# A gate's silu: by tanh on ScalarE and an operation on VectorE, or by ScalarE's own function

## The chip, the core and the metric

One core of a Trainium2 chip runs the whole program. The metric is the device time of one execution in microseconds; the median of 3 runs of the kernel before is 2064.26 us (2061.12 to 2065.25). Engines: TensorE (PE, with its weight loads as PEld), VectorE (DVE), ScalarE (ACT), GpSimd (POOL) and SyncE (SP), which issues most of the transfers.

## The reference

A decoder trunk of two layers on 512 tokens of width 1024, all in float32. A layer is a feed-forward, a mixer, a second feed-forward and an embedding step. This case is about the two feed-forwards:

```python
def swiglu(x, w_gate, w_up, w_down):
    return (jax.nn.silu(x @ w_gate) * (x @ w_up)) @ w_down   # 1024 -> 2816 -> 1024
h += 0.5 * swiglu(rmsnorm(h))                                # twice per layer
```

silu(g) is g times the sigmoid of g, which is the same as (g / 2) (1 + tanh(g / 2)). The mixer is a recurrent block, a windowed attention and a chunked delta rule side by side.

## The kernel before

Activations stand transposed, features on the partitions and the 512 tokens along the row. Every float32 operand of a matmul is split in two (a rounded part, `hi`, and the rest, `lo`) and a product takes three matmuls. ScalarE makes the `hi` parts by a copy, VectorE the `lo` parts by a subtraction; with the weights, which are split on the chip too, this is most of the work of both.

`ffn` computes the hidden 2816 columns as 11 pairs of 256. For a pair there are two *units*, first gate (`g`), then up (`u`). A unit computes a 256 by 512 block by seven quarter products (a fast matrix product) instead of eight; its sums gather in two PSUM banks, X and Y (`pg` and `qg`, `pu` and `qu` in the rows). ScalarE and VectorE read the banks (`c11`, L553 and L554: copy and add; `p37`, L558: a copy of Y; `p16`, L562; `c21`, L565; `c12`, L568) into a tile `cg` or `cu` of two halves. Half 1 of both comes with the sign turned. A product that adds onto a bank which is being read has to wait: the sixth waits for L554, the fourth for L558.

When both units of a pair are there, `Gating` takes over:

- `scale` (L496, VectorE): gate times the row norm
- `tanh(0)`, `tanh(1)` (L500, ScalarE): one half each, 128 x 512; the scale is 0.5 for half 0 and -0.5 for half 1
- `silu` (L503, VectorE): (tanh + 1) times the gate, both halves in one instruction of 128 x 1024; this is twice the silu, with the sign of half 1 turned
- `mult` (L506, VectorE): times `cu`, both halves in one instruction; the two signs cancel
- `hi` (L510, ScalarE) and `lo` (L513, VectorE): the split for the down product

The factor 2 left over is taken out in `residual` (L585), with the 1/2 of the layer: 0.25.

In the first feed-forward the first pair is done by plain products (`plain_pair`, `PlainGating`: L524, L528, the same L503, L532 in two halves). In the other three `first_pair` does it in an order of its own. The pairs go in two rounds, 5 and 6 of them, each followed by a part of the down product. The tile `cg` exists once: the next gate unit writes it (L553) after its last reader.

Inside the loops of units the order of TensorE, ScalarE and VectorE is the order of the code. The gating of a pair is spread over the next units: scale and the two tanh late in the up unit, `silu` and `mult` early and in the middle of the next gate unit. At the start of the three combined feed-forwards the first pair's scale, tanh, tanh and `silu` all come at once, in the first gate unit of the loop, ahead of that unit's weights (L449 adds two weight blocks, L443 subtracts) and of its L554. Outside these loops a planner orders ScalarE, VectorE, POOL and the DMA issues by simulated times; TensorE's order is by hand everywhere.

Of the kernel before, what the change touches and what calls it, by code (L numbers as in the profile page):

```python
# [14 lines left out]
AF = mybir.ActivationFunctionType  # L15
ALU = mybir.AluOpType
# [46 lines left out]
def trunk(ctx: ExitStack, tc: tile.TileContext, a):  # L63
    nc = tc.nc
    V, A, G, T = nc.vector, nc.scalar, nc.gpsimd, nc.tensor
# [291 lines left out]
    def ffn(l, which, at=AT1):  # L357
        with ExitStack() as es:
# [129 lines left out]
            class Gating:  # L488
# [7 lines left out]
                    V.tensor_tensor(out=self.cg, in0=self.cg, in1=rb, op=ALU.mult)  # L496
                    self.th = ft.tile([128, 2, S], F32, tag="th", name="th")

                def tanh(self, i):
                    A.activation(out=self.th[:, i, :], in_=self.cg[:, i, :], func=AF.Tanh, scale=0.5 - i)  # L500

                def silu(self):
                    V.scalar_tensor_tensor(out=self.th, in0=self.th, scalar=1.0, in1=self.cg, op0=ALU.add, op1=ALU.mult)  # L503

                def mult(self):
                    V.tensor_tensor(out=self.th, in0=self.th, in1=self.cu, op=ALU.mult)  # L506
                    self.out = self.hilo()

                def hi(self):
# [5 lines left out]
            class PlainGating(Gating):  # L515
# [8 lines left out]
                        V.tensor_tensor(out=self.cg[:, i, :], in0=self.ps["g", i], in1=norm.rb, op=ALU.mult)  # L524
                    self.th = ft.tile([128, 2, S], F32, tag="th", name="th")

                def tanh(self, i):
                    A.activation(out=self.th[:, i, :], in_=self.cg[:, i, :], func=AF.Tanh, scale=0.5)  # L528

                def mult(self):  # L530
                    for i in range(2):
# [50 lines left out]

            def residual(d, pd):
                dt = ft.tile([128, S], F32, tag="ys", name="dt", bufs=2)
                V.scalar_tensor_tensor(out=dt, in0=pd, scalar=0.25, in1=norm.rb, op0=ALU.mult, op1=ALU.mult)  # L585
                V.tensor_tensor(out=hT[:, d, :], in0=hT[:, d, :], in1=dt, op=ALU.add)

            units = [(j, m) for j in range(NP) for m in "gu"]
# [37 lines left out]
            norm, gain = yield  # L626
# [94 lines left out]
            for r, (j0, j1) in enumerate(ROUNDS):  # L721
                us = list(range(2 * j0, 2 * j1))

                t0 = (0, 10)[r]

                def chunk(d):
                    if d not in made:
                        made[d] = grouped(loaded(src[l, d][:, t0:t0 + 8, :], 8), 8)
                    return made[d]

                made = {}
                with tc.manual_schedule(engines=inner):
                    gate, last, pair, done = None, None, None, True
                    if r == 0:
                        gate, last, pair = plain_pair() if plain else first_pair()
                        us = us[2:]
                    for u in us:
                        for i in range(1, 4):
                            load2(u + i)
                        if u + 1 < 2 * j1:  # L740
                            load(u + 1)
                        if u + 2 < 2 * j1:
                            load(u + 2)
                        unit = Unit(*units[u], pipe.pop(u))
                        w = None
                        if u + 1 < 2 * j1:
                            w = pipe[u + 1] = Weights(u + 1)

                            w.room("a")
                            w.room("b")  # L750
                            w.hi("b")
                        else:
                            raws = [loaded(src[l, d][:, t0:t0 + 8, :], 8) for d in range(2)]
                        unit.p(2)
                        if unit.m == "g" and last:
                            if not pair:
                                pair = Gating(gate.c, last.c, into(r, last.j))
                                pair.scale()
                                pair.tanh(0)
                                pair.tanh(1)  # L760
                            pair.silu()
                        if unit.m == "u" and pair:
                            pair.lo()
                            pair = None
                        if w:
                            w.s2()
                            w.lo("b")
                        else:
                            made[0] = grouped(raws[0], 8)
                        unit.p(1)  # L770
                        unit.c11()
                        if w:
                            w.s4()
                        if not done:
                            last.p(5)
                            last.c12()
                        done = False
                        if w:
                            w.room("d")
                            w.hi("d")  # L780
                            w.hi("a")
                            w.lo("d")
                            w.lo("a")
                        else:
                            made[1] = grouped(raws[1], 8)
                        unit.p(3)
                        if pair and not last:
                            norm.rows()
                        unit.p(7)
                        if w:  # L790
                            w.room("c")
                            w.hi("c")
                        unit.p37()
                        if pair:
                            if not last:
                                pair.scale()
                                pair.tanh(0)
                                pair.tanh(1)
                                pair.silu()
                            pair.mult()  # L800
                        if unit.m == "u" and u + 1 < 2 * j1:
                            pair = Gating(gate.c, unit.c, into(r, unit.j))
                            pair.scale()
                        if w:
                            w.lo("c")
                        unit.p(6)
                        if unit.m == "u" and pair:
                            pair.tanh(0)
                        unit.p16()
                        if unit.m == "u" and pair:  # L810
                            pair.tanh(1)
                        if unit.m == "g" and pair:
                            pair.hi()
                        unit.p(4)
                        unit.c21()
                        if unit.m == "g":
                            gate = unit
                        last = unit
                    last.p(5)
                    last.c12()  # L820
                    pair = Gating(gate.c, last.c, into(r, last.j))
                    pair.scale()
                    pair.tanh(0)
                    pair.tanh(1)
                    pair.silu()
                    pair.mult()
                    pair.hi()
                    pair.lo()

                if r == 0:  # L830
                    ends = {}

                    def end(d):
                        e = d // 2
                        if e not in ends:
                            raw = wrp.tile([128, 4, 128], F32, tag="wr", name="wr")
                            for i in range(2):
                                nc.sync.dma_start(out=raw[:, 2 * i:2 * i + 2, :], in_=src[l, 2 * e + i][:, 8:10, :])
                            ends[e] = halfgroup()
                            split(raw, *ends[e])  # L840
                        i = 2 * (d % 2)
                        down(pds[d], ends[e], (i, i + 1), (8, 9), False, True)
                        residual(d, pds[d])

                    pds = {}
                    for d in range(KD):
                        pds[d] = bank([128, S], "pd")
                        chunk(d)
                        if d + 1 < KD:
                            chunk(d + 1)  # L850
                        if d == KD - 2:
                            load2(2 * j1)
                            load(2 * j1)
                            pipe[2 * j1] = Weights(2 * j1)
                            pipe[2 * j1].whole()
                        down(pds[d], chunk(d), range(8), range(8), True, False)
                        if d == 0:
                            continue
                        for e in ((0, 1) if d == 1 else (d,)):
                            end(e)  # L860
# [801 lines left out]
    norm = Norm(par[:, 0, C_F1:C_F1 + 8], True)  # L1662
# [28 lines left out]
    for l in range(L):  # L1691
        pl = par[:, l, :]
        norm = rest(f, norm, pl[:, C_MX:C_MX + 8])
        f = ffn(l, 2)
        norm = mixer(l, norm, pl[:, C_F2:C_F2 + 8], f)
# [126 lines left out]
```

## Time and profile before

| | |
|---|---|
| median of 3 runs | 2064.26 us |
| the profiled execution's own time | 2064.6 us |
| its span, first to last instruction | 2062.8 us |
| mean granted TensorE clock (1 is 2.4 GHz) | 0.977 |
| TensorE busy | 1975.7 us, 96% |
| VectorE busy | 1555.2 us, 75% |
| ScalarE busy | 996.1 us, 48% |
| POOL busy | 181.1 us, 9% |

Busy time is summed over the whole span. An engine that is 75% busy can be the limit in one stage and idle in another, so the stages are looked at one by one. `out<-in` names the tiles; the same line number stands for all instructions that a line of the kernel issues. An idle time in brackets is that of the engine before the instruction, with the one that ended it.

### The profile page before, as it was taken

What the parts mean: (1) busy time and instruction counts of PE and PEld (TensorE: products, weight loads), DVE (VectorE), ACT (ScalarE), POOL (GpSimd) and SP (SyncE); (2) the same over time, 40 slices, a digit from 0 to 9 for tenths busy, and PEclk for the clock granted to TensorE, in tenths of its full rate; (3) what the DMA queues carried; (4) which work ended last, traced back from release to release, by engine and by line L of the source; (5) the groups of instructions that cost most, each with busy time, mean ns of one, the idle gap of its engine ahead of it and who ended that gap; (6) DMA issues with size and microseconds to landing.
All of it is one profiled execution on the core that took longest, in us unless ns stands there. A gap on an engine that the chain in (4) does not pass through costs nothing.

```text
span 2062.8 us, 32001 instructions
## 1 busy us (share of the span) xinstructions
PE 1975.7 (96%) x12625; PEld 1759.0 (85%) x12625; DVE 1555.2 (75%) x2621; ACT 996.1 (48%) x1646; POOL 181.1 (9%) x197
## 2 busy tenths in 40 slices
PE   7999999999998999999989999999899999999996
PEld 5988998877678979997879899988676889899875
DVE  7975983879888857966879579657887888489466
ACT  5542652355655524543546346434365655155343
POOL 0000100052200000000001000000421000000001
PEclk8999999999999999999999999999899999999998
DMA  6763743211046735634357456322112367275411
GB/s 195 191 170 94 187 133 108 80 69 54 9 143 164 191 111 150 168 123 122 98 143 190 119 145 176 125 90 93 49 34 60 112 188 190 76 190 138 132 62 62
DMA packets 85415, 254.51 MB, mean 123 GB/s; under 512 B 9616, under 2 KB 17040, under 8 KB 85008
## 3 DMA queue, kind: packets, MB, share of 16 engines
q1 hardware_dynamic: 72880, 207.36, 30.8%
q0 software_dynamic: 12384, 45.09, 12.2%
q8 instruction: 99, 1.62, 0.3%
q14 instruction: 52, 0.43, 0.1%
HBM read 250.32 MB, written 2.10 MB: 122 GB/s over the span
## 4 chain that ended last, share of the span: by engine, by line
PE 77%; DVE 14%; ACT 5%; issue 3%; DMA 1%; POOL 0%; SPq 0%; DVEq 0%; ACTq 0%
PE pu L475 10%; PE pg L475 10%; PE qu L475 8%; PE pd L147 8%; PE pd L149 8%; PE pd L148 8%; PE qg L475 7%; PE pp L147 2%; PE pp L148 2%; PE pp L149 2%; DMA wr<-in_d_dram 1%; PE ppg L149 1%; PE ppg L148 1%; PE ppg L147 1%; DVE gl L443 1%
## 5 line engine op out<-in xcount | busy, mean ns | idle before, releaser
L475 PE MATMUL pu<-T,gh 128*128 128x256 f32 x880 | 159.5, 280 | 0.0
L475 PE MATMUL pg<-T,gh 128*128 128x256 f32 x784 | 144.4, 282 | 9.5 <-ACT T L251 7.5
L443 DVE TENSOR_TENSOR gl<-wr,gh 128x1024 fp32r<-128x1024 f32 x102 | 124.6, 1221 | 26.7 <-ACT gh L438 26.7
L123 ACT ACTIVATE wh<-wr 128x1024 fp32r<-128x1024 f32 (+2 forms) x76 | 77.2, 1015 | 133.4 <-PE pp L148 48.6
L475 PEld LDWEIGHTS pu<-T,gh 128*128 128x128 f32 x880 | 134.8, 188 | 0.0
L129 DVE TENSOR_TENSOR gl<-wr,gh 128x1024 fp32r<-128x1024 f32 x53 | 64.3, 1222 | 89.6 <-ACT gh L128 89.6
L475 PEld LDWEIGHTS pg<-T,gh 128*128 128x128 f32 x784 | 121.2, 189 | 11.1 <-ACT T L251 8.1
L147 PE MATMUL pd<-X,gh 128*128 128x512 f32 x328 | 128.8, 393 | 0.0
L149 PE MATMUL pd<-X,gl 128*128 128x512 f32 x328 | 128.4, 391 | 0.0
L148 PE MATMUL pd<-X,gh 128*128 128x512 f32 x328 | 128.1, 391 | 0.0
L475 PE MATMUL pu<-T,gl 128*128 128x256 f32 x440 | 123.2, 280 | 0.0
L475 PE MATMUL pg<-T,wh 128*128 128x256 f32 x592 | 108.3, 281 | 9.8 <-DVE cg L554 9.8
L438 ACT ACTIVATE gh<-wr 128x1024 fp32r<-128x1024 f32 x102 | 105.1, 1046 | 19.6 <-PE pd L148 14.1
L128 ACT ACTIVATE gh<-wr 128x1024 fp32r<-128x1024 f32 x53 | 55.8, 1058 | 119.8 <-PE pd L148 93.0
L475 PE MATMUL pg<-T,gl 128*128 128x256 f32 x392 | 110.3, 281 | 0.0
L124 DVE TENSOR_TENSOR wl<-wr,wh 128x1024 fp32r<-128x1024 f32 (+2 forms) x64 | 74.1, 1157 | 44.6 <-ACT wh L123 44.3
L438 ACT ACTIVATE sh<-r 128x512 fp32r<-128x512 f32 x80 | 50.7, 633 | 107.8 <-DVE r L455 107.8
L147 PE MATMUL pp<-X,wh 128*128 128x512 f32 x240 | 101.3, 422 | 0.0
L475 PEld LDWEIGHTS pg<-T,wh 128*128 128x128 f32 x592 | 91.3, 189 | 10.7 <-DVE cg L554 10.4
L443 DVE TENSOR_TENSOR wl<-wr,wh 128x1024 fp32r<-128x1024 f32 x67 | 81.8, 1221 | 23.3 <-ACT wh L438 23.3
L149 PE MATMUL pp<-X,wl 128*128 128x512 f32 x240 | 97.3, 406 | 1.0 <-DVE wl L124 1.0
L148 PE MATMUL pp<-X,wh 128*128 128x512 f32 x240 | 97.9, 408 | 0.2 <-DVE X L252 0.2
(475 smaller groups left out, 6109.0 us busy)
## 6 DMA issues: line engine op xcount, KB each, us to landing
wr<-in_d_dram SPq DMA_DIRECT2D x64, 512.0 KB, 3.8
wr<-in_g_dram SPq DMA_DIRECT2D x45, 512.0 KB, 4.2
wr<-in_u_dram SPq DMA_DIRECT2D x45, 512.0 KB, 4.1
r<-in_g_dram SPq DMA_DIRECT2D x43, 512.0 KB, 3.7
r<-in_u_dram SPq DMA_DIRECT2D x43, 512.0 KB, 3.8
r<-in_g_dram POOLq DMA_DIRECT2D x43, 512.0 KB, 7.3
r<-in_u_dram POOLq DMA_DIRECT2D x43, 512.0 KB, 7.0
wr<-in_wi_dram SPq DMA_DIRECT2D x30, 512.0 KB, 3.2
```

The lines of the kernel that those rows point to most:

```text
L123: A.activation(out=hi, in_=raw, func=AF.Copy)
L124: (via or V).tensor_tensor(out=lo, in0=raw, in1=hi.bitcast(F32), op=ALU.subtract)
L128: A.activation(out=hi, in_=x, func=AF.Copy)
L129: V.tensor_tensor(out=lo, in0=x, in1=hi.bitcast(F32), op=ALU.subtract)
L147: T.matmul(out=out, lhsT=wh, rhs=xh, start=start, stop=False)
L148: T.matmul(out=out, lhsT=wh, rhs=xl, start=False, stop=False)
L149: T.matmul(out=out, lhsT=wl, rhs=xh, start=False, stop=stop)
L438: A.activation(out=self.g[n][0], in_=self.of(n)[0], func=AF.Copy)
L443: V.tensor_tensor(out=g[1], in0=raw, in1=g[0].bitcast(F32), op=ALU.subtract)
L475: T.matmul(out=ps, lhsT=l_[:, q, :], rhs=r_, start=start and q == 0 and i == 0, stop=stop and q == 3 and i == 2, skip_group_check=more)
```

## The change

The tanh and the VectorE operation after it become one activation function per half. Since the silu now comes with its right sign in both halves and `cu` still has half 1 turned, `mult` is two instructions, the second with a factor -1. The factor in `residual` follows.

```diff
-                def tanh(self, i):
-                    A.activation(out=self.th[:, i, :], in_=self.cg[:, i, :], func=AF.Tanh, scale=0.5 - i)
-
-                def silu(self):
-                    V.scalar_tensor_tensor(out=self.th, in0=self.th, scalar=1.0, in1=self.cg, op0=ALU.add, op1=ALU.mult)
+                def silu(self, i):
+                    A.activation(out=self.th[:, i, :], in_=self.cg[:, i, :], func=AF.Silu, scale=1.0 - 2 * i)

                 def mult(self):
-                    V.tensor_tensor(out=self.th, in0=self.th, in1=self.cu, op=ALU.mult)
+                    V.tensor_tensor(out=self.th[:, 0, :], in0=self.th[:, 0, :], in1=self.cu[:, 0, :], op=ALU.mult)
+                    V.scalar_tensor_tensor(out=self.th[:, 1, :], in0=self.th[:, 1, :], scalar=-1.0, in1=self.cu[:, 1, :],
+                                           op0=ALU.mult, op1=ALU.mult)
...
-                    A.activation(out=self.th[:, i, :], in_=self.cg[:, i, :], func=AF.Tanh, scale=0.5)
+                    A.activation(out=self.th[:, i, :], in_=self.cg[:, i, :], func=AF.Silu)
...
-                V.scalar_tensor_tensor(out=dt, in0=pd, scalar=0.25, in1=norm.rb, op0=ALU.mult, op1=ALU.mult)
+                V.scalar_tensor_tensor(out=dt, in0=pd, scalar=0.5, in1=norm.rb, op0=ALU.mult, op1=ALU.mult)
...
-                                pair.tanh(0)
-                                pair.tanh(1)
-                            pair.silu()
+                                pair.silu(0)
+                                pair.silu(1)
```

At every other place `tanh(i)` becomes `silu(i)` and the call of `silu()` goes.

## Rows read from the trace of the kernel before

**Rows 1.** The page: busy time of TensorE; the chain that ended last, by engine

```profile
PE 1975.7 (96%) x12625; PEld 1759.0 (85%) x12625; DVE 1555.2 (75%) x2621; ACT 996.1 (48%) x1646; POOL 181.1 (9%) x197
...
PE 77%; DVE 14%; ACT 5%; issue 3%; DMA 1%; POOL 0%; SPq 0%; DVEq 0%; ACTq 0%
```

**Rows 2.** TensorE's waits, whole span: us in total, times, longest

```profile
PE pg L475 <- DVE cg L554: 9.8, 3, 3.5
...
PE qu L475 <- ACT ys L558: 7.9, 5, 2.1
```

**Rows 3.** Busy time by stretch: length, engines (instructions), granted clock, DMA share, GB/s

```profile
65.00:75.00 10.00, 8.07 (x69) 7.86 (x68) 9.56 (x14) 5.77 (x9) 0.86 (x1) 1.00 0.80 229
190.00:306.00 116.00, 115.60 (x981) 115.40 (x981) 99.88 (x123) 66.88 (x97) 6.92 (x8) 1.00 0.57 153
380.00:610.00 230.00, 219.86 (x1227) 175.60 (x1227) 191.19 (x506) 124.61 (x283) 50.93 (x50) 0.98 0.21 69
651.00:656.00 5.00, 4.45 (x23) 4.45 (x24) 4.01 (x5) 2.89 (x5) 0.86 (x1) 0.56 0.69 229
1069.00:1077.00 8.00, 6.65 (x43) 6.65 (x44) 6.75 (x8) 3.96 (x6) 0.86 (x1) 0.79 0.75 200
1390.00:1630.00 240.00, 228.73 (x1248) 182.22 (x1247) 196.53 (x522) 126.82 (x286) 51.83 (x51) 0.96 0.21 66
```

**Rows 4.** ScalarE in order of time, a steady unit: start, duration, idle before

```profile
804.65 0.39 ACT L553 ACTIVATE cg<-pg 128x256 f32<-128x256 f32 x1 [1.89 <-PE pg L475]
```

**Rows 5.** VectorE in order of time, the same unit

```profile
805.11 0.41 DVE L554 TENSOR_TENSOR cg<-cg,pg 128x256 f32<-128x256 f32 x1
```

**Rows 6.** VectorE, start of the second feed-forward of layer 0

```profile
642.13 1.22 DVE L496 TENSOR_TENSOR cg<-cg,rb 128x1024 f32<-128x1024 f32 x1
644.56 1.23 DVE L503 SCALAR_TENSOR_TENSOR th<-th,cg 128x1024 f32<-128x1024 f32 x1 [1.22 <-ACT th L500]
645.71 0.69 DVE L449 TENSOR_TENSOR wr<-r,wr 128x512 f32<-128x512 f32 x1
...
647.44 0.41 DVE L554 TENSOR_TENSOR cg<-cg,pg 128x256 f32<-128x256 f32 x1
```

**Rows 7.** ScalarE, the same start

```profile
643.38 1.15 ACT L500 ACTIVATE th<-cg 128x512 f32<-128x512 f32 x2 [2.06 <-DVE cg L496]
645.88 0.38 ACT L553 ACTIVATE cg<-pg 128x256 f32<-128x256 f32 x1 [1.35 <-DVE th L503]
...
650.92 0.57 ACT L558 ACTIVATE ys<-qg 128x512 f32<-128x512 f32 x1
```

**Rows 8.** TensorE, the first matmul after the wait at this start

```profile
647.91 0.39 PE L475 MATMUL pg<-T,wh 128*128 128x256 f32 x1 [3.46 <-DVE cg L554]
```

**Rows 9.** The chain that ended last, behind this start: start, us, what

```profile
651.55 2.93 PE qg L475 x12
654.48 3.29 PE pu L475 x24
```

**Rows 10.** The same chain, first feed-forward, behind the plain pair

```profile
58.33 1.24 DVE th L503
...
68.70 0.49 ACT ys L558
```

**Rows 11.** TensorE's waits from 60 to 75 us

```profile
PE qu L475 <- ACT ys L558: 1.9, 1, 1.9
```

**Rows 12.** ScalarE in the first mixer: a load of function tables

```profile
508.71 1.28 ACT L995 ACT_TABLE_LOAD   x1
```

**Rows 13.** POOL beside it: the operation whose result L995 reads

```profile
508.03 1.22 POOL L994 TENSOR_TENSOR g<-g,T 128x512 f32<-128x512 f32 x1 [5.58 <-ACT g L993]
```

**Rows 14.** Three lines' instructions: count, ns least/median/most, first and last start

```profile
L506 DVE TENSOR_TENSOR th<-th,cu x43: 1215/1218/1228, 78.4 to 1924.0; 128x1024 f32<-128x1024 f32 x43
...
L532 DVE TENSOR_TENSOR th<-th,pu x2: 680/683/686, 59.6 to 60.2; 128x512 f32<-128x512 f32 x2
...
L968 ACT ACTIVATE T<-pr,par x4: 684/686/687, 487.9 to 1505.5; 128x512 f32<-128x512 f32 x4
```

More of the change, by code (lines that the diff above doesn't have):

```diff
@@ L525, in scale, with silu @@
                     self.th = ft.tile([128, 2, S], F32, tag="th", name="th")
-                def tanh(self, i):
-                    A.activation(out=self.th[:, i, :], in_=self.cg[:, i, :], func=AF.Tanh, scale=0.5)
+                def silu(self, i):
+                    A.activation(out=self.th[:, i, :], in_=self.cg[:, i, :], func=AF.Silu)
                 def mult(self):
@@ L796, in ffn @@
                                 pair.scale()
-                                pair.tanh(0)
-                                pair.tanh(1)
-                                pair.silu()
+                                pair.silu(0)
+                                pair.silu(1)
                             pair.mult()
@@ L807, in ffn @@
                         if unit.m == "u" and pair:
-                            pair.tanh(0)
+                            pair.silu(0)
                         unit.p16()
                         if unit.m == "u" and pair:
-                            pair.tanh(1)
+                            pair.silu(1)
                         if unit.m == "g" and pair:
@@ L822, in ffn @@
                     pair.scale()
-                    pair.tanh(0)
-                    pair.tanh(1)
-                    pair.silu()
+                    pair.silu(0)
+                    pair.silu(1)
                     pair.mult()
```

## The prediction, made before the change was built

> **What bounds the kernel now.** I read the page's totals first, then the waits of the matrix engine, then the busy time by stage. In the totals TensorE is busy 96% of the span, VectorE 75%, ScalarE less than half; in the chain that ended last, 77% is TensorE and 14% VectorE [rows 1]. So removed VectorE work is worth something only where TensorE waits for it. The stretch from 190 to 306 us, nearly the twelve units of a feed-forward's second round, is the test: VectorE is busy 99.9 of 116 us, which looks near a limit, but TensorE is busy 115.6, so it waits for nobody [rows 3]. How it gets there can be seen at one unit of the same round in the next feed-forward: the first copy out of a product (L553) waits 1.89 us for TensorE, and the addition behind it (L554) starts as soon as that copy is done [rows 4, 5]. VectorE's queue is paced there by TensorE; an operation of 1.2 us taken out in front of L554 leaves a hole of 1.2 us and nothing else. Each of the four feed-forwards has such a stretch.
>
> The waits say where VectorE does end last. The largest line is matmuls of a unit's `pg` bank waiting for L554: 9.8 us in three waits, one at the start of each of the three feed-forwards that begin with `first_pair` [rows 2]. The next that touches the gate is `qu` waiting for the copy L558, five waits, of which one lies in the first feed-forward behind the plain pair's gating [rows 2, 11]; the other four are at round ends and behind a weight transfer.
>
> **The change part by part.**
>
> *The tanh becomes a silu on ScalarE.* 88 instructions of the same shape and place. The tanh pair takes 1.15 us [rows 7]. No row has a Silu; of this size a copy (L558) takes 0.57 us and a Sigmoid out of PSUM with a bias 0.69 [rows 7, 14], so two cost 1.1 to 1.4 us, and I take the tanh's 1.15.
>
> *The VectorE operation goes, at the three starts.* Take the second feed-forward of layer 0. VectorE does the scale (L496) at 642.13, then stands 1.22 us until the tanh is done, runs the silu operation (L503) at 644.56, and comes to L449 (work on the next weights) at 645.71 and to L554 at 647.44 [rows 6]. The bank's matmuls start at 647.91 after 3.46 us of waiting [rows 8]. Without L503 nothing in VectorE's queue needs the tanh at that place: L449 can start when the scale's slot ends. L503, of the same length, holds its slot from 644.56 to 645.71, 1.15 us; so that is 642.13 + 1.15 = 643.28, 2.43 us sooner than 645.71, and L554 then starts at 645.01. Its other input is the copy L553; in the old order that one waits for L503 too, 1.35 us [rows 7], since L503 is the last reader of the tile it writes. With L503 gone the last reader is the silu itself, on the same engine, done at 643.38 + 1.15 = 644.53, and the copy of 0.38 ends by 644.9. So L554 moves by the whole 2.43, and the wait of 3.46 becomes 1.0. What is late next is the copy L558, which releases the second bank: it ends at 651.49, 3.6 us behind L554's end, through L455, a half group and two groups on ScalarE, all in order behind L554 [rows 7]. It moves by 2.43 as well, so the matmuls that wait for it start at 649.1 instead of 651.55 [rows 9]. The twelve matmuls between take 1.41 us at the full clock (the steady stretch has 981 in 115.6 us [rows 3]), so TensorE will wait some 2.2 us there. Three starts: 3 x 2.43 = 7.3 us. If another input of L554 or L558 (a weight in flight) is late, the least is 0; nothing in the rows shows one.
>
> *The clock behind these waits.* After the two waits the next twelve matmuls take 2.93 us and the next 24 3.29, together 6.2 [rows 9], where 36 take 3 x 1.41 = 4.2: 2 us lost, at a mean granted clock of 0.56 from 651 to 656, so most of it at 1.2 GHz; at the start in layer 1 it is 0.79 over 8 us [rows 3]. Three starts: 6 us that could come back. Ahead of these falls TensorE had stood for 4.7 to 5.1 us in two waits; ahead of 65 to 75 us, with one wait of 1.9 us, the clock stays at 1.00 [rows 3, 11]. The new waits make 1.0 + 2.2 = 3.2, between the two. Ends 0 and 6; I take half, 3.
>
> *The plain pair in the first feed-forward.* Here L503 runs at 58.33 for 1.24 us on the chain, and behind it VectorE has no gap until the copy L558 at 68.70 [rows 10]. All of that moves 1.2 us forward, and the wait of 1.9 us [rows 11] becomes 0.7: 1.2 us.
>
> *The multiplication in two halves.* In 43 pairs one instruction of 1218 ns becomes two; two halves take 1.28 us where the plain pair already does so (683 and a slot of 0.60 ahead of it) [rows 14]; 0.06 us each. In steady stretches it lies in VectorE's hole. At four round ends it stands in front of the subtraction that frees a buffer for the next transfer: 4 x 0.06 = 0.2 us on the path. The one half as a scalar_tensor_tensor costs no more than the operation removed, which was one.
>
> *Function tables.* Silu is a function that the trace does not have. A load of tables takes 1.28 us here, and the one in front of L995 began at 508.71, while that line's operand was still being made on POOL until 508.03 + 1.22 = 509.25 [rows 12, 13]: it does not wait for the operand. I expect two more per layer, one Silu after a mixer and one Exp after a feed-forward. The Silu's falls into the 2.06 us that ScalarE idles before it at a start [rows 7], the Exp's into ScalarE's idle time in the down products. I take 0; with the cover gone, 4 x 1.28 = 5.1 us.
>
> The Trainium skill, "ScalarE: Activation LUTs", section "What ACT_TABLE_LOAD costs", states that a switch is about 2.66 us, a drain of 1.38 included. By that the four would be 10.6 us if exposed, and one Silu load would not fit in 2.06 us of idle time. The row has the load's 1.28 us alike; an exposed drain no row here shows.
>
> *The sum.* The profiled execution took 2064.6 us (2062.8 of span and 1.8 around it), 0.3 above the median of the runs. -7.3 - 3 - 1.2 + 0.2 + 0 = -11.3, so 2053.3 by the profile and 2053 by the median.
>
> **The rivals.**
>
> 1. *The clock falls all the same.* The two new waits stand close together, 3.2 us in about 4.7; that speaks for it, the 1.9 us without a fall against. Then the 3 us are not had: 2056.
>
> 2. *The loads are exposed.* For it: they are new, and the copies of a mixer's first operand run on the same engine. Against: the load that ran ahead of its operand. 2053 + 5 = 2058.
>
> 3. *The wait is only given another name.* At the starts the matmuls need L554's bank, then L558's, then the next unit's weights; if VectorE's lead is used up by weights that land no sooner, the 7.3 us come back as waits for transfers one unit on. For it: DMA engines are 0.69 to 0.75 busy in these stretches, against 0.57 in steady ones [rows 3]. Against: neither engine's rows there show a wait for a transfer. About 2064.
>
> 4. *Slower: the mixers are planned anew.* The order of VectorE, ScalarE and POOL outside the unit loops is written by a planner from its own estimate of times, and that estimate changes with the feed-forwards before it. The mixers are where TensorE depends on short chains: from 380 to 610 us it idles 230 - 219.9 = 10.1 us, from 1390 to 1630 us 240 - 228.7 = 11.3 [rows 3]. An order that doubled this costs 21.4 us: 2053 + 21 = 2074. It decides from 11.3 us on, half of that doubling; below, it only eats the gain. A better order is possible too, but can give back no more than the idle time. For it: nothing holds the order; against: the mixers' own work is unchanged.
>
> **How the numbers follow.** The forecast, 2053, 0.45, its own range 2048 to 2057 (all of the clock and none of it, with 1 us around). Rival 1 0.20, rival 2 0.10, rival 3 0.13, rival 4 0.12, of which 0.07 above its point by enough to be seen. A measurement of this kernel tells about 0.2% from no change, 4 us: faster means under 2060.1. The forecast and the first two rivals are under it (0.75, of which I give 0.01 back for their tails), rival 3 and the rest of rival 4 make 0.19 the same, 0.07 slower. The range is 2047 to 2064.5: a little under the full clock gain, up to rival 3.
>
> **What would show it.** The group L503 is gone; L449 follows L496 without a gap at the three starts; the waits for L554 add to some 3 us instead of 9.8, and those of `qg` for L558 grow by less than these fall; TensorE is as busy as before from 190 to 306 us while VectorE is down by about 5 us (five to six pairs at 1.1); the wait at 69 us is under 1 us; four table loads more, none with TensorE waiting behind it. If the three starts are shorter and the time is not, the mixers' idle time is the place. If the waits for L554 stay at 3 us each, my reading of its inputs was wrong.

## The result: 2052.0 us, and the profile after

The changed kernel takes 2052.02 us (median of 5 runs, 2047.78 to 2054.62) against 2064.26 (2061.12 to 2065.25): a ratio of 0.9943 [0.993, 0.9956]. Its profiled execution took 2052.9 us, 2051.1 of them span, at a mean granted clock of 0.980. These lines of its page answer to [rows 1]:

```profile
PE 1967.7 (96%) x12625; PEld 1752.2 (85%) x12625; DVE 1509.4 (74%) x2620; ACT 1002.0 (49%) x1651; POOL 181.2 (9%) x197
...
PE 75%; DVE 16%; ACT 4%; issue 3%; DMA 1%; SPq 0%; DVEq 0%; ACTq 0%
```

VectorE lost 45.8 us of work, and the span 11.8 (before rounding). L500 is now the silu, L504 and L505 the two halves of the multiplication; the lines from L507 to L758 are numbered as before, those of the mixers are lower by 3. TensorE's waits, for [rows 2]:

```profile
PE qg L475 <- ACT ys L558: 9.3, 8, 2.0
...
PE qu L475 <- ACT ys L558: 6.6, 5, 1.6
...
PE pg L475 <- DVE cg L554: 2.3, 3, 0.8
```

The line for L554 has left the top of this list; at the three starts the wait is 0.79, 0.73 and 0.79 us. The start of the second feed-forward of layer 0 on ScalarE, for [rows 7]:

```profile
645.40 1.28 ACT L500 ACT_TABLE_LOAD   x1
647.44 1.15 ACT L500 ACTIVATE th<-cg 128x512 f32<-128x512 f32 x2 [0.76 <-DVE cg L496]
648.63 0.38 ACT L553 ACTIVATE cg<-pg 128x256 f32<-128x256 f32 x1
...
652.54 0.57 ACT L558 ACTIVATE ys<-qg 128x512 f32<-128x512 f32 x1
```

On VectorE, for [rows 6]:

```profile
646.19 1.22 DVE L496 TENSOR_TENSOR cg<-cg,rb 128x1024 f32<-128x1024 f32 x1
647.33 0.68 DVE L449 TENSOR_TENSOR wr<-r,wr 128x512 f32<-128x512 f32 x1
...
649.06 0.41 DVE L554 TENSOR_TENSOR cg<-cg,pg 128x256 f32<-128x256 f32 x1
```

And the first matmuls behind the two waits on TensorE, for [rows 8], then the chain, for [rows 9]:

```profile
649.53 0.50 PE L475 MATMUL pg<-T,wh 128*128 128x256 f32 x2 [0.79 <-DVE cg L554]
...
653.17 0.51 PE L475 MATMUL qg<-T,wh 128*128 128x256 f32 x2 [2.01 <-ACT ys L558]
```
```profile
653.17 1.68 PE qg L475 x12
654.86 2.83 PE pu L475 x24
```

L449 follows the scale without a gap; from the scale to L554 it is 2.87 us, where it was 5.31 [rows 6]: 2.44 sooner. The silu has the tanh's 1.15 us. ScalarE is idle from 645.38 until the scale is done; the load takes 1.28 of these 2.06 us and leaves 0.76 idle. Behind the waits the 36 matmuls take 4.5 us instead of 6.2 [rows 9]: the clock did not fall.

The first feed-forward's plain pair is the exception. These are pieces of the chain that ended last there, for [rows 10]:

```profile
57.05 1.28 ACT L528
...
58.34 0.64 ACT th L528
...
68.12 0.49 ACT ys L558
```

A load of tables stands on that chain. Before, the tanh began at 57.07; now the silu begins at 58.34. The VectorE operation of 1.2 us is gone and a load of 1.28 has come. What is won is that the multiplication (L532) now begins behind the first half of the silu alone, at 59.01 instead of 59.59. There are fourteen loads now instead of nine; five are new, not four, and the fifth is this exposed one.

Where the 11.8 us of span went, by pieces between rows that both traces have (the norms' sums, L323, and the first `pg` matmul of each second round):

| piece | difference, us |
|---|---|
| up to the second round of the first feed-forward (with the plain pair) | -1.26 |
| from the norm to the second round, the three combined feed-forwards | -4.66 -1.70 -4.59 = -10.95 |
| from the first second round through the first mixer | +5.32 |
| from the other second rounds through the embedding step, through the second mixer and to the end | -1.58 -1.57 -1.75 = -4.90 |

The second line is the change. At each of the three starts the matmuls that wait for L558 begin 6.98 us behind the start of the scale (L496), where they began 9.42 us behind it: 2.44 sooner, 7.3 us in all. The 36 matmuls behind them take 14.6 us in sum over the three starts instead of 18.1: some 3.5 us, and that is the clock. (By name, the waits for L554 are 9.8 - 2.3 = 7.5 us shorter and those of `qg` for L558 1.3 us longer.) The first line can't be put down to the change: counted from the first norm's sums, this piece takes 146.4 us before and 145.2 after in these traces, but 148.5 and 148.0 in the second profiles of the same two kernels, which are described below. Ten microseconds from the first matmul behind the wait, at each of the three starts, before and then after (columns as in [rows 3]):

```profile
647.90:657.90 10.00, 8.79 (x51) 8.50 (x52) 8.04 (x9) 5.50 (x8) 0.86 (x1) 0.66 0.71 179
1066.70:1076.70 10.00, 7.98 (x53) 7.79 (x54) 7.94 (x9) 5.57 (x8) 0.86 (x1) 0.83 0.70 179
1664.70:1674.70 10.00, 8.47 (x49) 8.18 (x50) 8.06 (x9) 5.40 (x7) 0.86 (x1) 0.66 0.69 187
```
```profile
649.50:659.50 10.00, 7.96 (x65) 7.77 (x66) 9.05 (x13) 5.71 (x9) 1.29 (x2) 1.00 0.79 197
1062.00:1072.00 10.00, 7.91 (x52) 7.71 (x53) 8.18 (x11) 5.60 (x8) 1.73 (x2) 0.83 0.68 188
1656.80:1666.80 10.00, 7.93 (x65) 7.73 (x66) 9.05 (x14) 5.68 (x9) 0.86 (x1) 1.00 0.81 197
```

Two starts come back to 1.00 and one, the middle one, is at 0.83 in both. The other two lines of the table are +5.3 and -4.9. Up to the next norm's sums, with the second rounds and their changed gating in them, these four stretches agree within 0.2 us in the two traces (193.0 to 193.6 us each). The differences lie behind that, in the mixers and the embedding steps, where the change has no instruction; the first two experiments are about them.

### The profile page after: what moved, and what is told of

Its sections match the earlier page's. It is cut to its first block, busy times and chain, and to the rows that moved or that the text cites. A ratio compares the mean times of both kernels' runs of the same rounds, so it can differ in the third digit from the quotient of the medians.

```text
span 2051.1 us, 32033 instructions
## 1 busy us (share of the span) xinstructions
PE 1967.7 (96%) x12625; PEld 1752.2 (85%) x12625; DVE 1509.4 (74%) x2620; ACT 1002.0 (49%) x1651; POOL 181.2 (9%) x197
## 4 chain that ended last, share of the span: by engine, by line
PE 75%; DVE 16%; ACT 4%; issue 3%; DMA 1%; SPq 0%; DVEq 0%; ACTq 0%
PE pu L475 10%; PE pg L475 10%; PE pd L147 8%; PE pd L149 8%; PE qu L475 8%; PE pd L148 8%; PE qg L475 7%; PE pp L147 2%; PE pp L148 1%; PE pp L149 1%; PE ppg L149 1%; PE ppg L148 1%; PE ppg L147 1%; DVE wl L124 1%; DVE gl L443 1%
```

## Experiments

Theory: the gain is the start of the gating at the three combined feed-forwards, as a shorter wait and as a clock that does not fall behind it; the table loads are free only where ScalarE is idle. Rivals: the relief of VectorE over all pairs; another order in the mixers; loads that are free anyway. Kernels of one batch ran on one chip, beside the kernel before: the next four in one, then four, then three, then one.

**The kernel before, a second time** (no edit)

> The kernel before, unchanged, for a second profile. Theory (the mixers' differences between the two traces are only where the clock happened to fall): the first mixer, 248.7 us from one row of norm sums to the next in the trace of before, comes out elsewhere between 248 and 255 this time, and the stretches at a granted clock of 0.83 move or vanish. Rival (the planner's other order in the first mixer is worth its 5.3 us): the first mixer takes 248.7 +- 0.5 again. Both: the three waits for L554 are again 9.8 +- 0.5 us in sum.

**The changed kernel, a second time** (no edit)

> The changed kernel, unchanged, for a second profile. Theory (chance places of the clock's falls): the first mixer, 254.0 us in its first profile, moves by 1 to 5 us. Rival (order): 254.0 +- 0.5 again. Both: the three waits for L554 are 2.3 +- 0.5 us in sum again, and the three starts cost the same as in the first profile within 1 us.

They took 2067.35 and 2054.14 us, one execution each. The first mixer, from its norm's sums to the next: before, before again, after, after again (the column in front of the DMA share is the granted clock):

```profile
381.90:630.60 248.70, 237.28 (x1354) 191.68 (x1353) 207.82 (x536) 135.28 (x301) 52.64 (x52) 0.98 0.22 71
```
```profile
383.60:635.80 252.20, 239.90 (x1352) 193.49 (x1352) 207.82 (x535) 135.39 (x301) 52.55 (x52) 0.97 0.23 69
```
```profile
380.60:634.60 254.00, 241.56 (x1352) 195.30 (x1351) 208.02 (x535) 135.81 (x301) 52.73 (x52) 0.96 0.23 69
```
```profile
383.70:635.90 252.20, 239.37 (x1352) 193.06 (x1351) 208.71 (x536) 135.67 (x301) 52.58 (x52) 0.97 0.23 70
```

The same program takes 248.7 and then 252.2 us there, the other 254.0 and then 252.2, and the clock column goes with it. The planner did write another order for the small operations of this mixer, but the second looks agree to 0.1 us: the 5.3 us are not the order's. The -4.9 us are no better founded. The embedding step between the layers, 73.2 us before and 71.5 after in the first profiles, takes 73.4 and 73.3 in the second ones; the second mixer takes 253.8 and 252.1 us before, 252.1 and 249.7 after; and a step at the end, 50.0 before and 48.4 after, is 48.4 in a kernel with the tanh (TensorE kept busy) and 50.0 in one with the silu (VectorE's queue). The waits for L554 were 9.8 and 2.2 us again.

The second profiles also change the picture of the clock. Ten microseconds from the first wait at the middle start, before again and after again:

```profile
1072.00:1082.00 10.00, 7.99 (x66) 7.79 (x67) 9.05 (x12) 5.86 (x9) 0.86 (x1) 1.00 0.69 183
```
```profile
1065.80:1075.80 10.00, 8.00 (x52) 7.80 (x53) 8.14 (x10) 5.63 (x8) 0.95 (x2) 0.83 0.79 204
```

The kernel before keeps 1.00 there this time. Over all traces whose starts still have the wait for L558, including those of the experiments below (the kernel with TensorE kept busy left out), the first and third starts are at 0.66 whenever the wait for L554 is about 3 us (four traces) and at 1.00 whenever it is about 0.8 (five traces, one of them with 1.1 us at the third). At the middle start it is the other way round: 0.83 in all five with the short wait, 1.00 in three of the four with the long one. So the change gives the clock back at two starts and, more often than not, takes some at the middle one: over the three starts the 36 matmuls take 16.7 us before again and 14.6 after again, 2.1 us less and not 3.5.

**Silu for the first pairs only**

The flag is set where a start makes its pair, and in `PlainGating`; the rest of the kernel is that of before, with its factor of 0.25.

```diff
-pair = Gating(gate.c, last.c, into(r, last.j))
+pair = Gating(gate.c, last.c, into(r, last.j), True)
...
-A.activation(out=self.th[:, i, :], in_=self.cg[:, i, :], func=AF.Tanh, scale=0.5 - i)
+if self.own:
+    A.activation(out=self.th[:, i, :], in_=self.cg[:, i, :], func=AF.Silu, scale=1.0 - 2 * i)
+else:
+    A.activation(out=self.th[:, i, :], in_=self.cg[:, i, :], func=AF.Tanh, scale=0.5 - i)
...
+if self.own:
+    for i in range(2):
+        V.scalar_tensor_tensor(out=self.th[:, i, :], in0=self.th[:, i, :], scalar=2.0 - 4 * i,
+                               in1=self.cu[:, i, :], op0=ALU.mult, op1=ALU.mult)
```

> Silu by ScalarE only for the first pair of each of the four feed-forwards (the plain one among them); all other pairs keep tanh and the VectorE operation. Theory (the gain sits at the starts): 2052 us +- 4, the three waits for L554 2.3 us in sum, five more table loads or so. Rival (relief of VectorE over all pairs): about 2063 us. VectorE's busy time falls by only some 5 us of the 46 that the change took off, by both.

**Silu for all the others**, the complement

The flag `old` is set at the same places, in the changed kernel.

```diff
+if self.old:
+    A.activation(out=self.th[:, i, :], in_=self.cg[:, i, :], func=AF.Tanh, scale=0.5 - i)
+    if i == 1:
+        V.scalar_tensor_tensor(out=self.th, in0=self.th, scalar=1.0, in1=self.cg, op0=ALU.add, op1=ALU.mult)
...
+if self.old:
+    V.scalar_tensor_tensor(out=self.th, in0=self.th, scalar=0.5, in1=self.cu, op0=ALU.mult, op1=ALU.mult)
```

> The other part alone: Silu by ScalarE for every pair but the first of each feed-forward, which keep tanh and the VectorE operation of 1.1 us. Theory (starts): 2064 us +- 4, waits for L554 again 9 to 10 us in sum. Rival (relief of VectorE): 2053 us. If the clock's falls in the mixers follow the order: somewhere between, with the first mixer's time saying which.

First pairs only: 2051.65 us, 0.9954 [0.9939, 0.997], VectorE busy 1550.9. All the others: 2064.63 us, 1.0003 [0.9993, 1.0013], VectorE busy 1515.6. TensorE's waits for the addition L554 (L565 and L564 here), first pairs only and then all the others:

```profile
PE pg L475 <- DVE cg L565: 2.2, 3, 0.8
```
```profile
PE pg L475 <- DVE cg L564: 9.6, 3, 3.3
```

Four pairs of the 44 carry the gain. The other 40 took off 39.6 us of VectorE's work, 1555.2 - 1515.6, for nothing that the times show (by the interval 1.4 us at most).

**More table loads at the starts**

```diff
 pair = Gating(gate.c, last.c, into(r, last.j))
+A.activation(out=junk[:, 0:1], in_=zero, func=AF.Sqrt)
+A.activation(out=junk[:, 1:2], in_=zero, func=AF.Exp)
 pair.scale()
```

> The changed kernel with two tiny activations (Sqrt and Exp of one column, nobody reads them) ahead of the first pair's Silu at the three combined starts, so that three table loads stand there where there were one, one and none. ScalarE was idle for 2.04 us there, of which the one load took 1.28. Theory (the load was free because the idle time covered it): three loads and two small activations, some 4.3 us, stick out by 2.2 us per start, 6.6 in all, and the clock falls again behind the longer wait: 2059 us (2057 to 2063), waits for L554 9 us in sum. Rival (a load runs beside the engine's work and never costs): 2052 us +- 3, waits for L554 2.3 us.

2062.72 us, 0.9996 [0.9987, 1.0005]: the whole gain is gone. ScalarE at the second feed-forward of layer 0 (its lines are one higher), then TensorE's wait there:

```profile
642.51 1.04 ACT L439 ACTIVATE gh<-r 128x1024 fp32r<-128x1024 f32 x1
643.57 1.28 ACT L759 ACT_TABLE_LOAD   x1
644.86 0.20 ACT L759 ACTIVATE junk<-warm 128x1 f32<-128x1 f32 x1
645.07 1.28 ACT L760 ACT_TABLE_LOAD   x1
646.36 0.20 ACT L760 ACTIVATE junk<-warm 128x1 f32<-128x1 f32 x1
646.57 1.28 ACT L501 ACT_TABLE_LOAD   x1
647.87 1.15 ACT L501 ACTIVATE th<-cg 128x512 f32<-128x512 f32 x2
```
```profile
PE pg L476 <- DVE cg L555: 3.4, 1, 3.4
```

The scale was done at 645.58, so the silu is 2.29 us late, 2.2 expected, and the wait is 3.4 us instead of 0.8. In the three times 10 us behind the waits the clock is 0.66, 1.00 and 0.66. A load is on ScalarE's path like any instruction, and the cover at a start is two microseconds. The Trainium skill, "ScalarE: Activation LUTs", section "What ACT_TABLE_LOAD costs", adds a drain of 1.38 us to a load of 1.28. The rows agree on the load and show no drain: each load begins 0.01 to 0.02 us behind the end of the instruction before it, and the activation after it 0.01 to 0.02 us behind its end.

**The kernel before, with TensorE kept busy in the waits**

```diff
 unit.p(7)
+start = r == 0 and not plain and u == us[0]
+if start:
+    keep = bank([128, S], "keep")
+    for i in range(14):
+        T.matmul(out=keep, lhsT=warm, rhs=warm[:, 0:1].to_broadcast([128, S]), start=True, stop=True)
...
+if start:
+    for i in range(8):
+        T.matmul(out=keep, lhsT=warm, rhs=warm[:, 0:1].to_broadcast([128, S]), start=True, stop=True)
 unit.p(4)
```

> The kernel before with 14 and 8 small matmuls of zeros that nobody reads in TensorE's two idle times at each of the three combined starts, none of them longer than the idle time by the rows (14 x 0.21 = 3.0 of 3.5 us, 8 x 0.21 = 1.7 of 2 us). The waits stay, the idleness goes. Theory (behind the wait the clock fell since TensorE was idle, 2.93 instead of 1.68 us for twelve matmuls): the matmuls behind the waits run at full clock, and the sum falls by 3 to 5 us, to 2060 us. Rival (the clock falls there whatever stands in the idle time): 2064 to 2066 us and 2.9 us for the twelve again.

2059.24 us, 0.998 [0.9969, 0.9991]. At the first of the starts, on TensorE (one of the 14 records is missing), and then ten microseconds behind the first wait at all three:

```profile
648.94 3.22 PE L794 MATMUL keep<-warm 128*128 128x512 bf16 x13
652.34 0.50 PE L475 MATMUL pg<-T,wh 128*128 128x256 f32 x2 [0.18 <-DVE cg L554]
...
653.81 1.91 PE L821 MATMUL keep<-warm 128*128 128x512 bf16 x8
655.98 0.51 PE L475 MATMUL qg<-T,wh 128*128 128x256 f32 x2 [0.26 <-ACT ys L558]
```
```profile
652.30:662.30 10.00, 9.71 (x73) 8.46 (x74) 9.05 (x12) 5.78 (x9) 0.86 (x1) 1.00 0.65 156
1071.30:1081.30 10.00, 9.74 (x76) 8.45 (x76) 9.04 (x12) 5.77 (x9) 0.86 (x1) 1.00 0.70 180
1666.50:1676.50 10.00, 9.77 (x73) 8.51 (x74) 9.05 (x12) 5.80 (x9) 0.86 (x1) 1.00 0.65 177
```

Data came as late as before: the matmuls that wait for L558 begin 9.42 to 9.43 us behind the start of the scale. Yet the clock stays at 1.00 at all three starts, the 36 matmuls take 12.9 us in sum, and the time falls by 4.9 us without any work being saved. So the clock is a price of its own, behind the wait, and without TensorE's idleness it is not paid here.

**The next wait: ys copied ahead at the starts**

ScalarE's copies of the next weights are `hi("d")`, `hi("a")` and, behind `p(7)`, `hi("c")`; `p(3)`, `p(7)` and `p37` no longer follow further down for this unit.

```diff
+soon = r == 0 and not plain and u == us[0]
+if soon:
+    unit.p(3)
+    unit.p(7)
+    unit.p37()
 if w:
     w.room("d")
     w.hi("d")
     w.hi("a")
```

> The changed kernel, where at the three combined starts ScalarE copies ys (L558) ahead of the three copies of the next weights instead of behind them. Theory (the wait that took the place of the one removed is order on ScalarE's queue): the three waits of qg for L558, 2.0 us each now, go, and the time falls by 5 to 9 us with the clock: 2045 us (2042 to 2048). Rival (the weights' copies are as urgent): the next unit waits for its weights instead, 2052 us +- 2.

**The same at the round ends**

```diff
-soon = r == 0 and not plain and u == us[0]
+soon = not w or (r == 0 and not plain and u == us[0])
```

> As the kernel before this one, and at the four round ends ScalarE copies ys ahead of splitting the down projection's second block of weights, whose transfer it waits for. Theory: the waits of qu for L558, 1.6 us at each of four round ends, go too: 2039 us (2035 to 2044). Rival (the down projection waits for its weights instead): as the kernel before this one, within 2 us.

Both miss. At the starts: 2049.69 us, 0.9931 [0.9919, 0.9944], where 2045 was expected. TensorE's wait for L558 at the second feed-forward of layer 0, and ScalarE:

```profile
PE qu L475 <- ACT ys L558: 1.0, 1, 1.0
```
```profile
646.90 0.59 ACT L558 ACTIVATE ys<-qg 128x512 f32<-128x512 f32 x1
...
657.46 0.63 ACT L438 ACTIVATE sh<-r 128x512 fp32r<-128x512 f32 x1 [3.00 <-DVE r L455]
...
659.89 0.57 ACT L558 ACTIVATE ys<-qu 128x512 f32<-128x512 f32 x1
```

The wait of 2.0 us is gone, and one of 1.0 us stands a unit later, for the other bank; ScalarE idles 3 us there for VectorE. At the round ends: 2052.12 us, 0.9949 [0.9937, 0.996]. ScalarE at the end of a round:

```profile
720.53 0.63 ACT L128 ACTIVATE sh<-wr 128x512 fp32r<-128x512 f32 x1 [4.72 <-DMA wr<-in_d_dram]
721.07 0.58 ACT L558 ACTIVATE ys<-qu 128x512 f32<-128x512 f32 x1
```

The copy was moved ahead of one split of the down projection's weights, and stands behind another that also waits for its transfer. The wait is now for another transfer.

**VectorE's queue in the second unit**, with the two kernels to compare on the same chip

```diff
-if unit.m == "u" and pair:
+late = unit.m == "u" and r == 0 and not plain and u == us[1]
+if unit.m == "u" and pair and not late:
     pair.lo()
...
 w.lo("d")
+if late:
+    pair.lo()
+    pair = None
 w.lo("a")
```

> The changed kernel once more, timed on the same chip as the two that follow. All theories: 2052 us +- 2 beside 2064 of before.

> The kernel with ys copied ahead at the three starts, again, beside the changed kernel. Theory (its three waits of 2.0 us came back as 1.0 us one unit later, since VectorE is busy without a gap from the pair's gating on): 1.0 us each stays won, 3 us, so 2049 us. Rival (nothing is won, its 2.3 us were noise): the same as the changed kernel within 1 us.

> As the one before it, and in the second unit after a start VectorE forms the pair's low part (L513, 1.22 us, read only at the round's end) behind the sum that ScalarE waits for (L455) instead of ahead of it. Theory (VectorE's queue is what the second unit waits for): L455 and the copy of ys come 1.2 us earlier, the three waits of qu for L558 (1.0 us each) go, 2046 us (2044 to 2049). Rival (the weights' transfer or ScalarE's copies set it): the waits stay at 1.0 us, 2049 us.

2053.95 us (0.9951 [0.9937, 0.9966]), 2051.84 (0.9936 [0.9924, 0.9948]) and 2050.46 (0.9941 [0.9928, 0.9954]). The rows follow the theory in the last one; TensorE's wait at the start of 1.0 us:

```profile
PE qu L475 <- ACT ys L558: 0.3, 1, 0.3
```

At the other two starts it is gone. So VectorE's queue is what the second unit waited for. The times do not settle it: the three intervals overlap, and the clock's falls alone moved the first mixer by 1.8 and 3.5 us between executions of one program. No version is shown to beat the change.

**The load in front of the plain pair, taken earlier**

```diff
 w.room("d")
+if plain and r == 0 and u == us[0]:
+    A.activation(out=junk[:, 0:1], in_=zero, func=AF.Silu)
 w.hi("d")
```

> The changed kernel with one tiny Silu (one column, nobody reads it) put on ScalarE of the first feed-forward ahead of the copies of the next weights, where ScalarE idles 2.75 us, so that the load of Silu's tables in front of L528 (1.28 us, at 57.05 to 58.33 on the chain that ended last) comes there instead. Theory (this load, the fifth, stands on the path: without it the plain pair's silu starts 1.28 us sooner): L528 starts behind ys without a load, VectorE goes from the scale (L524) to L532 after some 0.2 us instead of 1.43, the wait of qu for L558 falls from 1.4 to about 0.2 us, and the time falls by 1.2 us, which is below what the times can tell. Rival (the operand of the silu was late anyway): L528 starts at 58.3 as before and the wait stays 1.4 us.

2051.9 us, 0.9939 [0.9915, 0.9963]. ScalarE (lines one higher):

```profile
52.17 1.28 ACT L781 ACT_TABLE_LOAD   x1
53.47 0.20 ACT L781 ACTIVATE junk<-warm 128x1 f32<-128x1 f32 x1
...
57.81 0.58 ACT L559 ACTIVATE ys<-qg 128x512 f32<-128x512 f32 x1
58.38 1.23 ACT L529 ACTIVATE th<-gs 128x512 f32<-128x512 f32 x2
```

The silu follows ys without a load; VectorE goes from the scale's start (57.66) to the multiplication's (59.04) in 1.38 us, where the changed kernel takes 2.72, 56.29 to 59.01. The wait of `qu` for L558 is no longer among TensorE's waits from 50 to 75 us. The load was exposed there, by its whole 1.3 us; in the times that does not show.

## Why the prediction was right

The forecast was 2053.0 and the runs gave 2052.0, by the steps that it named, with one of them wrong and hidden by its size, and with some luck in the term for the clock.

- *The operation at the three starts*, 7.3 us: VectorE reached L554 2.44 us sooner, 2.43 forecast, and the matmuls behind L558 moved by the same 2.44 at all three, 7.3 us. Doing the first pairs alone gives the gain, doing the others alone gives none.
- *Late next*: `qg` waits for L558, 2.2 us forecast and 2.0 measured. In sum these three went from 4.7 to 6.0 us, so they grew by less than the others fell.
- *The clock*, half of 6 us: some 3.5 came back in the first pair of profiles, as all of it at two starts and nothing at the middle one, and 2.1 in the second pair, where the middle start had not fallen before. Half was about the right sum for the wrong picture, and that is luck. That the clock is separate from the wait was an inference; the matmuls of zeros showed it, with 4.9 us.
- *The hole in steady stretches*: in the same stretch of the trace after, from 188.7 to 304.7 us, VectorE is busy 94.8 us, 5.1 less than [rows 3], and TensorE 115.6 as before.
- *Function tables, taken as 0*: this step failed at one place. I expected four more loads, two per layer, and there is a fifth in front of the plain pair, where nothing covers it. There *the plain pair*'s 1.2 us was mis-sized: its copy L558 came 0.5 us sooner and the wait went from 1.9 to 1.4 us, not under 1. With the load moved away it came 1.8 us sooner than before, counted from the L554 ahead of it, and the wait was gone. The 1.26 us by which this stage is shorter in the first pair of traces are no evidence, since it differs by 2 to 3 us between two profiles of one kernel. At the other starts the cover was real, and three loads in its place cost all of the gain.
- *The multiplication in halves*, 0.2 us: 684 ns per half, as assumed; nothing this small shows in the times.
- *The rivals*. The clock fell all the same at one start of three. One new load was exposed. The wait was not given another name by a transfer. The mixers' order was written anew, and cost nothing that the second profiles confirm.

The two sums of some 5 us outside the starts, of opposite sign, nearly cancel in the first pair of traces. Had I compared the two mixers and stopped, I would have found a loss that is none.

## What to carry to other kernels

Work taken off an engine that is 75% busy was worth its time in 3 places of 44, those where the matrix engine waited for it; in a fourth a table load took its place, and the same edit in the other 40 was worth nothing that could be measured. A wait of the matrix engine had two prices here, its length and the slower clock that can follow, and a wait that went left part of itself to the next one: with L554's gone the waits for L558 grew by 1.3 us, and with those gone one of 1.0 us stood a unit later. Count a new function's table loads at every place where the function follows another set, and name the idle time that covers each; a difference between two traces in a stage that was not touched wants a second profile of both before it gets a cause.

## What was not expected of the hardware

- The clock behind two starts of the same shape differs: waits of 0.79 and 2.01 us left it at 1.00, 0.73 and 2.01 us at the middle start were followed by 0.83. There longer waits were followed by 1.00: 3.05 and 2.01 us in the second profile of the kernel before, 2.86 and 1.96 with more loads. The length of the wait alone does not decide, and what does stays open.
- L500 has two loads, both behind a mixer. The second layer's first feed-forward, the middle start, needs none (the expectation for more loads has the third there), though the tanh of the embedding step (L1614) stands between: in these runs the two functions shared their tables.
- One and the same program differs by 3.5 us in one mixer between two executions, with the clock at 0.98 and 0.97.
